# Gate projections moved from the output stage into attention, V products in groups, output stage pipelined deeper

## The chip, the core and the metric

The kernel runs on one core of a Trainium2 chip. The metric is device time in microseconds (us) of one execution, 4000.34 us before the change. TensorE multiplies matrices (PE in the profile; PEld is its loading of stationary operands), VectorE is DVE, ScalarE is ACT, GpSimd is POOL, and SyncE (SP) issues the DMAs.

## The reference, cut to what matters

Two layers of a mixer over 2048 latent and 256 context tokens of width 1024. A layer norms and modulates the stream, projects it, runs four branches of width 256 side by side, gates each by SiLU(z) of the same projection, and projects back:

```
h = rms_norm(x, g) * (1 + sc) + sh
(aq, ak, av, az, bq, bk, bv, bz, cu, cv, cz, dq, dk, dv, dz, drf, drb) = split(h @ w_in)
ya = rms_norm over heads of (softmax(q1 k1) - lam softmax(q2 k2)) v      # A: 4 heads
yb = softmax(q k) v, grouped queries                                     # B: 4 heads, 2 of k and v
yc = u * (w_s layer_norm(v) + b_s)                                       # C: in chunks of 128 tokens
yd = rms_norm(gated linear attention forwards + backwards)               # D
x  = x + gt * ([ya silu(az), yb silu(bz), yc silu(cz), yd silu(dz)] @ w_out)
```

The last layer gives no context output, and a final RMS norm follows.

## The kernel before, in words

All tokens are cut into 18 tiles of 128 (2 of context, 16 of latents; 34 tiles over both layers have an output, 18 and 16). Dense products are taken to float32's accuracy as three float32r products: `mm3` (lines 99 to 105) multiplies the two parts of h (hh, hl) with the two parts of a weight, over 8 row tiles, so 24 products per 512 columns. Each layer has four stages.

`proj_attn` and `proj_cd` compute h, q, k, v and the branches C and D but for D's backward scan; `pa_front` writes h to DRAM as `hT`, and `h_tile` (line 326) reads it back and splits it again into hh and hl, with a copy on ScalarE and a subtraction on VectorE (`split_tile`, line 284).

`attention` (line 743) goes through 4 rounds (a head of A together with one of B) of 8 blocks of 256 queries against all 2304 keys; in layer 0 each round has a small block for the context in front. `Slots` emits the work in slots, 18 per full block, in which blocks overlap. In a slot stands a score chunk of 768 keys: two products (`da_chunk`, line 845; `g_chunk`, line 883) into a PSUM tile s of two banks (two buffers), and one instruction of VectorE that reads it, keeps the scores of A and their running extreme. Then `da_exp` (858) exponentiates a whole row of 2304 on ScalarE, and `da_comb` subtracts the second softmax: 512 columns by ScalarE and POOL (871, 872), the others on VectorE in two pieces of 896 (875). In the slots of the next block follow `tr` (905, four transposes and a copy on ScalarE), `gs` (917 to 920, the transposed scores of B, an exponential on ScalarE, and a sum `acc` of them on POOL, 926), both through the PSUM tiles b (three buffers), and `pvm` (937), the V products: A's and B's halves write 64 partitions each, so they use 64 columns of TensorE's array (128*64 in the rows; other products have 128*128). One V product stands as four instructions in the trace. `o1` to `o3` scale and store a block's result `ot` (944 to 970). The order on TensorE is the scheduler's here: it places instructions by priority and its own cost model. SyncE's queue issues all loads in order; a load waits there for its buffer.

`output` (line 1070) takes the tiles in reverse, as D's backward scan does. Per tile it multiplies h with the gates' weights (two `mm3` of 512 columns, `pz`), norms A and D (`mixers`), multiplies with SiLU(pz) (`gates`), transposes (`turned`) and multiplies with w_out (two `mm3`, `po`, in `project`), which a tile later than the gates. TensorE's order is the order of the program there (`manual_schedule`). The first half of the gates' weights and the first tile of h are loaded while the last block of attention ends (1047 to 1059).

Of the kernel before, what the change touches and what calls it, by code (L numbers as in the profile page):

```python
# [9 lines left out]
F32 = mybir.dt.float32  # L10
F32R = mybir.dt.float32r
# [20 lines left out]
BIG = 3.0e38  # L32

# columns of the input projection
# [17 lines left out]
class Slots:  # L52
    """Emission in the order of slots, so that blocks overlap."""
# [17 lines left out]

class Kernel:
# [26 lines left out]
    def mm3(self, ps, hh, hl, wh, wl, c0, c1, ks=range(KT)):  # L99
        """ps = (hh + hl)^T (wh + wl) to float32's accuracy, over row tiles ks of KT."""  # L100
# [6 lines left out]
    def weights(self, wp, name, widths):  # L107
        """Tiles for the two parts of weights; the first are laid where a pool before frees its first."""
# [28 lines left out]
    # ---------------------------------------------------------------- all  # L137
    def run(self):
        tc, nc, I = self.tc, self.nc, self.I
        self.table()  # L140
        with ExitStack() as cx:
# [6 lines left out]
            # per layer: (1 + sc) g and sh by feature, lambda  # L148
# [16 lines left out]
            for i in range(DEPTH):  # L165
                d = {}
                for n, s in (
                    ("hT", [NTILE, P, KT * P]), ("aqk", [512, 2, NT]), ("bqk", [384, 2, NT]), ("v", [NT, 384]), ("o", [NT, 512]), ("c", [NT, 256]), ("od", [NT, 256]),
# [39 lines left out]
    # ---------------------------------------------------------------- modulation  # L208
    def ada(self, i, parts, wp, pp, start=False):
        """Shift (0), scale (1) and gate (2) of layer i, in steps of about a tile of weights."""  # L210
        nc, I = self.nc, self.I
        NB = 256
        if 2 in parts:
            # lambda, negated
# [11 lines left out]
        for r in parts:  # L226
# [33 lines left out]
            else:  # L260
                # rms_norm leaves out the factor 32 = sqrt(1024), which is put here
# [30 lines left out]
    def pa_load(self, i, t):  # L292
        """Tile t of the stream, normed (but for gains), and its rotary factors."""
# [12 lines left out]
    def pa_front(self, i, t, xn, pt, tag):  # L306
        """Tile t modulated and transposed, in two float32r parts."""
# [16 lines left out]
        nc.sync.dma_start(out=self.D[i]["hT"][t], in_=hT.rearrange("p k t -> p (k t)"))  # L324
        return self.split_tile(hT)

    def h_tile(self, i, t):
        """The same, from memory."""
        hT = self.xp.tile([P, KT, P], F32, name="hT", tag="hT", bufs=1)
        self.nc.sync.dma_start(out=hT.rearrange("p k t -> p (k t)"), in_=self.D[i]["hT"][t])  # L330
        return self.split_tile(hT)

    def pa_weights(self, i):
        """Weights of q and k of A, and of q, k and v of B."""
# [8 lines left out]
    def proj_attn(self, i, X, H, wcx, W):  # L343
        nc, I, D = self.nc, self.I, self.D[i]
        last = i == DEPTH - 1
        with ExitStack() as cx:
# [29 lines left out]
            for t in range(NTILE):  # L376
# [10 lines left out]
                def part_a():  # L387
                    """A: q, k"""
# [7 lines left out]
                def part_b():  # L396
                    """B: q, k, v"""
# [19 lines left out]
                def part_v():  # L417
                    """A: v"""
# [13 lines left out]
                else:  # L432
                    # the longer chain first
# [22 lines left out]
    def proj_cd(self, i, wc, first):  # L456
        nc, I, D = self.nc, self.I, self.D[i]
        last = i == DEPTH - 1
        with ExitStack() as cx:
# [19 lines left out]
            # C's constants  # L479
# [9 lines left out]
            # D's constants  # L489
            # rows: hi, hi and lo of the low-rank weights, hi and lo of the bias  # L490
# [30 lines left out]
            def stages(t, B):  # L521
                """The chain of one tile's D and C; each stage begins with work of TensorE."""
# [4 lines left out]
                # q, k and the decays' low-rank part, transposed  # L527
# [15 lines left out]
                # log-decays, both directions: min(z, 0) - ln(1 + exp(-|z|)); the 1 / 16 is in tri  # L543
# [11 lines left out]
                # their sums within the chunks: up to a token (transposed), and behind it  # L555
# [30 lines left out]
                # state increments of both directions, the forward scan  # L586
# [28 lines left out]
                # scores within the chunks, both directions  # L615
# [16 lines left out]
                if t % 2:  # L632
                    # C: the mix over the chunk's positions, two chunks at once
# [14 lines left out]
                # D: within the chunks, and from the state before  # L648
# [37 lines left out]
            # the chains of tiles without output are run behind, as they have less between their stages  # L686
# [55 lines left out]
    # ---------------------------------------------------------------- branches A and B  # L742
    def attention(self, i):
# [4 lines left out]
        CH, NCH = 768, 3  # L748
        with ExitStack() as cx:
            dcx = ExitStack()  # L750
            dp = dcx.enter_context(self.pool(f"dk{i}", 5, side="right"))
            qp = cx.enter_context(self.pool(f"qp{i}", 3))
            kp = cx.enter_context(self.pool(f"kp{i}", 2))
            ep = cx.enter_context(self.pool(f"ep{i}", 7))
# [584 lines left out]
```

## Time and profile before

| | |
|---|---|
| runs | 4000.34 us median of 3 (3998.8 to 4002.73) |
| span of the profiled execution | 4001.6 us, 67227 instructions; no other time of it is on the page |
| busy over the span | PE 3883.3 us (97%), DVE 2730.4 (68%), ACT 2322.1 (58%), POOL 1461.5 (37%) |
| DMA | 339.21 MB, mean 85 GB/s |
| mean granted clock of TensorE | 0.983 |

A layer's stages from the span's start: projections to 668 us, attention to 1640, output to 2062, projections to 2660, attention to 3605, output to the end. Busy times are unions of an engine's instructions. TensorE's instructions overlap each other in the records, so what one costs is read from the distance between the starts of two, not from its duration.

### The profile page before, as it was taken

The page shows a single profiled execution, that of the slowest core. Times are in us where ns is not written, and L with a number is a line of the kernel's source. Part 1 is how long each engine was busy: PE and PEld are TensorE (multiplying, and loading weights), DVE is VectorE, ACT ScalarE, POOL GpSimd, SP SyncE. Part 2 cuts the span into 40 slices and gives each one's busy share as a digit, 9 for nine tenths or more (in the row PEclk, how much of TensorE's full clock was granted, in tenths as well). Part 3 has the DMA queues.
Part 4 walks back from the last instruction along what each step waited for, and adds up shares of the span by engine and source line. Part 5 has one row for each costly group of instructions (what it writes and reads, how often), then busy time and mean ns, then how long its engine had stood idle before and what let it go on. Part 6 is the DMA issues. An engine that isn't in the chain of part 4 may idle for free.

```text
span 4001.6 us, 67227 instructions
## 1 busy us (share of the span) xinstructions
PE 3883.3 (97%) x24276; PEld 2877.1 (72%) x24276; DVE 2730.4 (68%) x6088; ACT 2322.1 (58%) x4181; POOL 1461.5 (37%) x1454
## 2 busy tenths in 40 slices
PE   7999998999999999999999999989999999999999
PEld 5888885666666666677878888866666666667777
DVE  5555545898989889533346654468999999976443
ACT  4434444677777777634444434447777777766554
POOL 1223221555555555311111132225555555552111
PEclk9999998999999999999999999979999999999999
DMA  8444334211020100533235431141111201015321
GB/s 265 148 150 133 115 99 111 65 41 43 22 67 21 33 24 24 182 103 104 94 120 179 143 119 56 60 106 49 45 34 29 56 21 31 22 50 169 103 95 58
DMA packets 302795, 339.21 MB, mean 85 GB/s; under 512 B 99384, under 2 KB 245760, under 8 KB 302464
## 3 DMA queue, kind: packets, MB, share of 16 engines
q1 hardware_dynamic: 302464, 334.92, 27.7%
q8 instruction: 192, 3.15, 0.3%
q14 instruction: 139, 1.14, 0.1%
HBM read 234.15 MB, written 100.62 MB: 84 GB/s over the span
## 4 chain that ended last, share of the span: by engine, by line
PE 87%; DMA 4%; DVE 4%; issue 2%; ACT 2%; POOL 1%; SPq 1%; DVEq 0%; POOLq 0%; ACTq 0%
PE pv L937 16%; PE s L845 8%; PE b L905 7%; PE b L917 5%; PE s L883 4%; PE b L918 3%; PE pz L103 3%; PE po L103 3%; PE po L105 3%; PE pz L105 3%; PE pz L104 3%; PE po L104 3%; PE pc L103 2%; PE pc L105 2%; PE pc L104 2%
## 5 line engine op out<-in xcount | busy, mean ns | idle before, releaser
L926 POOL TENSOR_TENSOR acc<-acc,gp 128x512 f32<-128x512 f32 x448 | 711.2, 1587 | 465.4 <-ACT gp L920 455.6
L937 PE MATMUL pv<-gp,v 128*64 128x256 f32 x2320 | 709.6, 400 | 0.0
L937 PE MATMUL pv<-wt,v 128*64 128x256 f32 x2320 | 709.2, 400 | 0.0
L858 ACT ACTIVATE e<-e,dm 128x2304 f32<-128x2304 f32 x256 | 568.7, 2221 | 48.3 <-DVE e L850 48.3
L850 DVE TENSOR_SCALAR_CACHE_REDUCE e<-s,dm 128x768 f32<-128x768 f32 x512 | 509.3, 1012 | 97.4 <-PE s L845 96.6
L845 PE MATMUL s<-dak,daq 128*128 128x384 f32 (+1 forms) x1568 | 461.8, 377 | 17.4 <-DMA daq<-aqk 7.4
L875 DVE SCALAR_TENSOR_TENSOR e<-e,r 128x896 f32<-128x896 f32 x256 | 457.8, 1808 | 0.1
L920 ACT ACTIVATE gp<-b 128x512 f32<-128x512 f32 x580 | 345.7, 596 | 100.5 <-PE b L918 87.9
L909 ACT COPY wt<-b 128x512 f32<-128x512 f32 x580 | 338.5, 585 | 112.5 <-PE b L905 99.0
L937 PEld LDWEIGHTS pv<-gp,v 128*64 128x64 f32 x2320 | 236.8, 135 | 205.8 <-issue 142.6
L905 PE MATMUL b<-ident,e 128*128 128x128 f32 x2304 | 360.7, 278 | 1.2 <-POOL e L872 1.2
L917 PE MATMUL b<-qa,ka 128*128 128x256 f32 x1160 | 354.2, 321 | 0.2
L905 PEld LDWEIGHTS b<-ident,e 128*128 128x128 f32 x2304 | 269.6, 141 | 93.7 <-issue 53.9
L845 PEld LDWEIGHTS s<-dak,daq 128*128 128x128 f32 x1568 | 247.7, 197 | 106.0 <-issue 85.5
L918 PE MATMUL b<-qb,kb 128*128 128x256 f32 x1160 | 305.5, 281 | 0.0
L917 PEld LDWEIGHTS b<-qa,ka 128*128 128x128 f32 x1160 | 220.7, 190 | 97.2 <-issue 71.6
L872 POOL TENSOR_TENSOR e<-e 128x512 f32<-128x512 f32 x128 | 171.2, 1337 | 306.5 <-ACT e L871 306.2
L888 DVE TENSOR_SCALAR_CACHE_REDUCE junk<-s,gm 128x768 bf16<-128x768 f32 x256 | 259.6, 1014 | 31.3 <-PE s L883 21.0
L850 DVE TENSOR_SCALAR_CACHE_REDUCE e<-s 128x768 f32<-128x768 f32 x256 | 239.6, 952 | 49.1 <-PE s L845 48.9
L1195 POOL TENSOR_TENSOR x<-x,g 128x512 f32<-128x512 f32 x66 | 88.8, 1345 | 427.1 <-DVE g L1193 406.4
L937 PEld LDWEIGHTS pv<-wt,v 128*64 128x64 f32 x2320 | 237.0, 135 | 0.6 <-issue 0.3
L883 PE MATMUL s<-ka,qa 128*128 128x384 f32 (+1 forms) x784 | 227.6, 373 | 9.1 <-DVE junk L888 6.2
(289 smaller groups left out, 9127.5 us busy)
## 6 DMA issues: line engine op xcount, KB each, us to landing
hT<-hT SPq DMA_DIRECT2D x104, 512.0 KB
dak<-aqk SPq DMA_DIRECT2D x96, 192.0 KB
daq<-aqk SPq DMA_DIRECT2D x136, 128.0 KB
wst<-in_w_in_dram SPq DMA_DIRECT2D x64, 256.0 KB
xa<-in_ada_w_dram SPq DMA_DIRECT2D x32, 512.0 KB
bst<-bst SPq DMA_DIRECT2D x68, 194.0 KB
xa<-xb SPq DMA_DIRECT2D x19, 512.0 KB
v<-v SPq DMA_DIRECT2D x16, 576.0 KB
```

The costliest lines, as they stand in the source:

```text
L845: nc.tensor.matmul(s[:, u, :hc], lhsT=Q["daq"][m][:, qt * P : (qt + 1) * P], rhs=R["dak"][m][c][:, u * hc : (u + 1) * hc], start=True, sto ...
L850: nc.vector.tensor_scalar(out=E[qt, m][:, c * ch : (c + 1) * ch].rearrange("p (u f) -> p u f", u=2), in0=s[:, :, :hc], scalar1=-SC, scalar ...
L858: nc.scalar.activation(e, e, AF.Exp, bias=NM[qt, m], scale=-1.0, accum_out=L[qt][:, m : m + 1])
L875: nc.vector.scalar_tensor_tensor(out=E0[:, a : a + w], in0=E1[:, a : a + w], scalar=RR[qt][:, 2:3], in1=E0[:, a : a + w], op0=ALU.mult, op ...
L883: nc.tensor.matmul(s[:, u, :hc], lhsT=Q["QA"][:, qt * P : (qt + 1) * P], rhs=R["KA"][c][:, u * hc : (u + 1) * hc], start=True, stop=True,)
L905: nc.tensor.transpose(s[:, j * 256 + qt * P : j * 256 + (qt + 1) * P], W[qt][:, k * P : (k + 1) * P], ident)
L909: nc.scalar.copy(WT[u], s)
L917: nc.tensor.matmul(o, lhsT=R["KA"][k // 6][:, ks], rhs=Q["QA"], start=True, stop=False)
L918: nc.tensor.matmul(o, lhsT=R["KB"][k // 6][:, ks], rhs=Q["QB"], start=False, stop=True)
L920: nc.scalar.activation(g, s, AF.Exp, scale=0.125)
L926: nc.gpsimd.tensor_tensor(out=B["acc"], in0=B["acc"], in1=g, op=ALU.add)
L937: nc.tensor.matmul(B["pv"][o : o + 64, :256], lhsT=R["V"][:, k, o : o + 64], rhs=x[:, js], start=k == 0, stop=k == nkt - 1,)
```

## The change

The gates' products become a generator, `gates`, which goes through the four branches' weights (256 columns each) and all output tiles, and yields after every product of 256 columns; each finished piece is copied out by ScalarE and stored in DRAM as `z`. A class `Pace` draws from it: at two places in each slot of attention, `fill` takes products until a counted cost reaches `rate` times the slot. The counts (352 for a chunk, 432 for `tr`, 472 for `gs`, 432 for `pvm`, 119 for a gate product) are nanoseconds. h is stored in DRAM as its two parts (`hs`), and `h_tile` reads these without splitting.

In attention TensorE now follows the program's order. V products are emitted in four groups per block, of the pairs of key tiles (0, 1), (2, 3), (4, 5) and (6, 7, 8). The combination is wholly VectorE's, in four pieces; the exponential goes in two halves of a row; the four scalings of a result become one instruction. The PSUM tiles b have two buffers instead of three, as `pz` takes a bank. Buffers of k, v and the score rows are fewer, v comes in halves, loads stand elsewhere in their slots, and a round's blocks run from the last to the first. The first half of w_out is loaded at the end of attention.

The output stage reads z, applies SiLU from SBUF, and lets `mixers` run two tiles ahead of `project`; `turned` has two pairs of buffers, `po` three banks.

```diff
@@ new, beside Slots
+STEP = 119
+class Pace:
+    def __init__(self, steps, n, slots, cost):
+        self.steps, self.left, self.cost, self.rest = steps, n, 0, 0
+        self.rate = (n * STEP + cost) / slots
+    def fill(self, slot):
+        if slot < 3 or slot < self.rest:
+            return
+        for _ in range(8):
+            if not self.left or self.cost >= self.rate * slot:
+                return
+            self.step(slot)
+    def step(self, slot):
+        if next(self.steps) is None:
+            self.rest = slot + 1
+            return
+        self.left -= 1
+        self.cost += STEP
@@ h_tile
-        hT = self.xp.tile([P, KT, P], F32, name="hT", tag="hT", bufs=1)
-        self.nc.sync.dma_start(out=hT.rearrange("p k t -> p (k t)"), in_=self.D[i]["hT"][t])
-        return self.split_tile(hT)
+        h = []
+        for z, n in enumerate(("hh", "hl")):
+            h.append(self.xp.tile([P, KT, P], F32R, name=n, tag=n))
+            self.nc.sync.dma_start(out=h[z].rearrange("p k t -> p (k t)").bitcast(F32), in_=self.D[i]["hs"][t, :, z])
+        return h
@@ attention
-            pb = cx.enter_context(self.pool(f"pb{i}", 3, PSUM))
+            pb = cx.enter_context(self.pool(f"pb{i}", 2, PSUM))
+            pz = cx.enter_context(self.pool(f"pz{i}", 1, PSUM))
+            cx.enter_context(self.tc.manual_schedule(engines={PE}))
...
+                    pace.cost += 352 if full else 120
...
-                def da_exp(qt, m):
-                    e = E[qt, m][:, :nk]
-                    nc.scalar.activation(e, e, AF.Exp, bias=NM[qt, m], scale=-1.0, accum_out=L[qt][:, m : m + 1])
+                def da_exp(qt, m, b):
+                    w = nk // 2
+                    e = E[qt, m][:, b * w : (b + 1) * w]
+                    nc.scalar.activation(e, e, AF.Exp, bias=NM[qt, m], scale=-1.0, accum_out=L[qt][:, b, m : m + 1])
...
-                        if npl:
-                            nc.scalar.activation(E1[:, :npl], E1[:, :npl], AF.Copy, scale=r[:, 2:3])
-                            nc.gpsimd.tensor_tensor(out=E0[:, :npl], in0=E0[:, :npl], in1=E1[:, :npl], op=ALU.add)
...
-                    for qt in range(2):
-                        for o, sc in ((0, RR[qt][:, 0:1]), (64, rl[:, 2 * qt : 2 * qt + 1])):
-                            dst, src = ob[:, qt, o : o + 64], op[:, qt * P + o : qt * P + o + 64]
-                            nc.vector.tensor_scalar(out=dst, in0=src, scalar1=sc, scalar2=None, op0=ALU.mult)
+                    nc.vector.tensor_tensor(
+                        out=ob.rearrange("p t (b d) -> p t b d", d=64),
+                        in0=B["op"][:, 0:256].rearrange("p (t b d) -> p t b d", t=2, d=64),
+                        in1=bc(B["r"][:, :, 0:2], [[4, 2], [1, 2], [0, 64]]), op=ALU.mult,
+                    )
...
-                        S.at(s + 1 + 2 * m, lambda qt=qt, m=m: da_exp(qt, m), -1)
-                    npt = 2 if full else 1
+                        for b in range(2):
+                            S.at(s + 1 + 2 * m + b, lambda qt=qt, m=m, b=b: da_exp(qt, m, b), -1)
+                    npt = 4 if full else 1
...
+                for z in range(int(base), int(s)):
+                    S.at(z, lambda z=z: pace.fill(z), 3)
+                    S.at(z, lambda z=z: pace.fill(z + 0.5), 9)
...
-                        for j in range(2):
-                            S.at(b0 + 2 * u + 5.5 + j, lambda u=u, j=j: pvm(u, j), 5)
+                    for us in ((0, 1), (2, 3), (4, 5), (6, 7, 8)):
+                        for u in us:
+                            for j in range(2):
+                                S.at(b0 + 2 * us[-1] + 5.5, lambda u=u, j=j: pvm(u, j), 5)
...
-                for b in range(8):
+                for b in reversed(range(8)):
+            pace = Pace(self.gates(i, fp, pz), 24 * 4 * (NTILE if with_ctx else NTILE - CTILE), 32 * 18 + with_ctx * 12, 32 * 25200 - 17000)
@@ new
+    def gates(self, i, fp, pz):
...
+        def load():
+            t, b = halves[len(loaded)]
+            h = fp.tile([P, 2, KT // 2, P], F32R, name="fh", tag="fh", bufs=3)
...
+        for n, (g, t) in enumerate(units):
+            ps = pz.tile([P, 512], F32, name="pz", tag="pz")
+            for k in range(KT):
+                if k % 4 == 0 and len(loaded) < len(halves):
+                    load()
+                h = loaded[2 * n + k // 4]
+                w = W[g, k]
+                for z, (a, b) in enumerate(((0, 0), (0, 1), (1, 0))):
+                    nc.tensor.matmul(
+                        ps[:, :256], lhsT=h[:, a, k % 4], rhs=w[:, b], start=k == 0 and z == 0, stop=k == KT - 1 and z == 2
+                    )
+                    yield 1
+                if t == tiles[-1] and g < 3:
+                    weight(g + 1, k)
+            zs = fp.tile([P, 256], F32, name="zs", tag="zs", bufs=2)
+            nc.scalar.copy(zs, ps[:, :256])
+            nc.sync.dma_start(out=D["z"][t * P : (t + 1) * P, g * 256 : (g + 1) * 256], in_=zs)
+            yield None
@@ output
-                self.mm3(B["pz"][0], hh, hl, *Wz[0], 0, 512)
...
+            chain(0)
+            turned(T[0])
+            chain(1)
+            chain(2)
+            for k, (n, b) in enumerate(steps):
+                if k + 1 in firsts.values():
+                    turned(T[steps[k + 1][0]])
+                if b == 0 and n > 0:
+                    chain(n + 2)
+                project(T[n], b)
```

`chain(n)` is `mixers` of tile n and the scan and loads of the next; `steps` are the pairs (tile, half of w_out).

## Rows read from the trace of the kernel before

**Rows 1.** Busy time of each engine by stage; instructions in brackets, then clock, DMA.

```profile
330.00:668.00 338.00, 331.60 (x2747) 268.17 (x2746) 168.56 (x520) 157.63 (x482) 90.69 (x202) 1.00 0.33 107
668.00:1640.00 972.00, 948.58 (x6196) 628.95 (x6196) 846.37 (x1676) 687.99 (x1055) 505.86 (x365) 0.98 0.17 45
1640.00:2062.00 422.00, 418.10 (x1944) 331.93 (x1944) 172.75 (x391) 188.77 (x251) 77.86 (x118) 0.99 0.34 112
...
3605.00:4001.00 396.00, 383.08 (x1768) 302.10 (x1768) 183.32 (x438) 209.16 (x296) 70.66 (x108) 0.98 0.32 105
```

The busy times are in the order PE, PEld, DVE, ACT, POOL.

**Rows 2.** The same for ten blocks of layer 1's attention.

```profile
2800.00:3083.30 283.30, 282.18 (x1882) 188.75 (x1884) 257.34 (x493) 207.69 (x310) 158.99 (x111) 1.00 0.13 35
```

**Rows 3.** Groups by line, same ten blocks: busy us, mean ns, idle before.

```profile
L875 DVE SCALAR_TENSOR_TENSOR e<-e,r 128x896 f32<-128x896 f32 x40 | 74.3, 1876 | 0.0
...
L964 DVE TENSOR_SCALAR ob<-b,rl 128x64 f32<-128x64 f32 x20 | 5.5, 274 | 0.0
...
L858 ACT ACTIVATE e<-e,dm 128x2304 f32<-128x2304 f32 x40 | 88.9, 2222 | 4.2 <-DVE e L850 4.2
...
L909 ACT COPY wt<-b 128x512 f32<-128x512 f32 x90 | 52.6, 585 | 14.5 <-PE b L905 12.1
...
L944 ACT COPY ot<-pv 128x256 f32<-128x256 f32 x10 | 3.7, 373 | 3.5 <-PE pv L937 3.5
```

**Rows 4.** TensorE's timeline, 3000 to 3029.6 us: start, duration, instruction.

```profile
3001.07 0.43 PE L937 MATMUL pv<-gp,v 128*64 128x256 f32 x1
...
3002.53 0.38 PE L937 MATMUL pv<-gp,v 128*64 128x256 f32 x1
...
3002.75 0.38 PE L937 MATMUL pv<-gp,v 128*64 128x256 f32 x1
...
3010.49 0.53 PE L845 MATMUL s<-dak,daq 128*128 128x384 f32 x2
3010.85 0.28 PE L917 MATMUL b<-qa,ka 128*128 128x256 f32 x1
3010.97 0.27 PE L918 MATMUL b<-qb,kb 128*128 128x256 f32 x1
3011.18 0.43 PE L937 MATMUL pv<-gp,v 128*64 128x256 f32 x1
...
3011.76 0.63 PE L845 MATMUL s<-dak,daq 128*128 128x384 f32 x2
3012.22 0.60 PE L905 MATMUL b<-ident,e 128*128 128x128 f32 x4
...
3026.58 0.43 PE L937 MATMUL pv<-gp,v 128*64 128x256 f32 x1
```

**Rows 5.** TensorE's timeline in an output stage and in a projection stage.

```profile
1849.98 0.39 PE L104 MATMUL pz<-zl,hh 128*128 128x512 f32 x1
...
1855.09 0.40 PE L105 MATMUL pz<-zh,hl 128*128 128x512 f32 x1
...
2499.89 0.28 PE L103 MATMUL pqk<-cwh,hh 128*128 128x256 f32 x1
...
2500.84 0.28 PE L105 MATMUL pqk<-cwh,hl 128*128 128x256 f32 x1
```

**Rows 6.** Groups by line on ScalarE, layer 1's output stage.

```profile
L288 ACT CAST hh<-hT 128x1024 fp32r<-128x1024 f32 x15 | 15.6, 1041 | 0.0
```

**Rows 7.** The chain that ended last, end of layer 0's attention: start, us, what.

```profile
1634.92 4.49 DMA wst<-in_w_in_dram
```

**Rows 8.** Line 875's instructions in layer 1: duration in ns, min/median/max.

```profile
L875 DVE SCALAR_TENSOR_TENSOR e<-e,r x128: 1139/2054/2181, 2679.1 to 3579.1; 128x896 f32<-128x896 f32 x128
```

**Rows 9.** Timelines of POOL and VectorE, 2821.5 to 2827 us.

```profile
2822.07 1.30 POOL L872 TENSOR_TENSOR e<-e 128x512 f32<-128x512 f32 x1 [2.48 <-ACT e L871]
...
2822.13 4.26 DVE L875 SCALAR_TENSOR_TENSOR e<-e,r 128x896 f32<-128x896 f32 x2
```

**Rows 10.** Waits of SyncE's queue in layer 0's attention: us, times, longest.

```profile
SPq L818 <- PE s L845: 308.5, 24, 14.4
```

More of the change, by code (lines that the diff above doesn't have):

```diff
@@ L69, in run, with begin, drain @@
                 f()
+class Pace:
+    def __init__(self, steps, n, slots, cost):
+        self.steps, self.left, self.cost, self.rest = steps, n, 0, 0
+        self.rate = (n * STEP + cost) / slots
+    def begin(self):
+        next(self.steps)
+    def fill(self, slot):
[11 more added lines that the diff above has]
+        self.cost += STEP
+    def drain(self):
+        for _ in self.steps:
+            pass
 class Kernel:
@@ L837, in da_chunk @@
                         E[qt, m] = (
[L838 removed]
+                            ep.tile([P, NT], F32, name=f"e{m}", tag=f"e{m}", bufs=4 - 2 * m) if full
                             else ep.tile([P, 256], F32, name="ec", tag="ec", bufs=5)
@@ L880, in g_chunk @@
                 def g_chunk(qt, c):
+                    pace.cost += 352 if full else 120
                     s = pf.tile([P, 2, 512], F32, name="s", tag="s")
@@ L900, in tr @@
                 def tr(u):
+                    pace.cost += 432
                     s = pb.tile([P, 512], F32, name="b", tag="b")
@@ L911, in gs @@
                 def gs(u):
+                    pace.cost += 472
                     s = pb.tile([P, 512], F32, name="b", tag="b")
@@ L932, in pvm @@
                     k = 2 * u + j
+                    pace.cost += 432
                     if k == 0:
@@ L1022, in attention @@
                 ld_dak(R, c)
+            pace.begin()
             for c in range(with_ctx, NCH):
                 ld_ka(R, c)
-            ld_v(R)
+            for c in range(2):
+                ld_v(R, c)
             for bi, (r, q0, nk) in enumerate(blocks):
@@ L1046, in attention @@
                 base = end
+            pace.drain()
             dcx.close()
@@ L1070, in output @@
-    def output(self, i, zcx, Wz, turn):
+            gcol = hp.tile([P, 2], F32, name="gcol")
+            lam_init = 0.8 - 0.6 * math.exp(-0.3 * i)
+            for j, n in enumerate(("da_subln_g", "gla_norm_g")):
+                for o in (0, 64):
+                    nc.sync.dma_start(out=gcol[o : o + 64, j : j + 1], in_=self.I[n][i].rearrange("(p o) -> p o", o=1))
+            nc.vector.tensor_scalar(out=gcol[:, 0:1], in0=gcol[:, 0:1], scalar1=1.0 - lam_init, scalar2=8.0, op0=ALU.mult, op1=ALU.mult)
@@ L1071, in output, with out_weights @@
+    def out_weights(self, i, W, b, gcol, stage=None):
+        for k in range(KT):
+            col = gcol[:, 0:1] if k < 2 else gcol[:, 1:2] if k >= 6 else None
+            src = self.I["w_out"][i, k * P : (k + 1) * P, b * 512 : (b + 1) * 512]
+            self.split_weights(W[0][:, k, :], W[1][:, k, :], [src], 512, col, stage)
+    def output(self, i, zcx, Wo, gcol):
         nc, I, D = self.nc, self.I, self.D[i]
         last = i == DEPTH - 1
-        lam_init = 0.8 - 0.6 * math.exp(-0.3 * i)
@@ L1172, in turned, with project @@
                     nc.vector.tensor_tensor(out=yl[:, ks], in0=p3, in1=yh[:, ks].bitcast(F32), op=ALU.subtract)
-            def project(t, B, mid=None):
+            def project(B, b):
+                t = B["t"]
                 s = 1 if t < CTILE else 0
                 ts = slice(t * P, (t + 1) * P)
+                end = last and t == outs[-1]
                 if s not in gts:
@@ L1229, in output @@
[L1229 to L1250 removed]
+            bsts = [scan(t) for t in order[: order.index(outs[0]) + 1]][-1:]
@@ new lines, in output, with chain @@
+            T = [load(t) for t in outs[:2]]
+            Wo = Wo + self.weights(wo, "ob", [512])
+            self.out_weights(i, Wo[1], 1, gcol)
+            cx.enter_context(self.tc.manual_schedule(engines={PE}))
+            def chain(n):
+                if n < NO:
+                    mixers(bsts[n], T[n])
+                if n + 1 < NO:
+                    bsts.append(scan(outs[n + 1]))
+                    if n + 1 >= len(T):
+                        T.append(load(outs[n + 1]))
+            steps = [(0, 0), (1, 0), (0, 1), (1, 1)]
@@ new lines, in output @@
+            tail = 0 if last else 2
+            steps += [(n, b) for n in range(2, NO - tail) for b in range(2)]
+            if tail:
+                steps += [(NO - 2, 0), (NO - 1, 0), (NO - 2, 1), (NO - 1, 1)]
+            firsts = {n: k for k, (n, b) in enumerate(steps) if b == 0}
+            chain(0)
+            turned(T[0])
+            chain(1)
+            chain(2)
+            pw = None
+            for k, (n, b) in enumerate(steps):
[4 more added lines that the diff above has]
+                project(T[n], b)
+                if not last and (n, b) == (NO - 1, 0):
+                    zcx.close()
+                    pw = self.pa_weights(i + 1)
+                    self.tc.keep_in_program_order(self.table())
+                    X, H = {t: self.pa_load(i + 1, t) for t in range(2)}, {}
+                if not last and (n, b) == (NO - 2, 1):
+                    H[0] = self.pa_front(i + 1, 0, X[0][0], pt, "py")
```

225 lines of the change are left out of this document (92 added, 133 removed).

## The prediction, made before the changed kernel was run

> **What bounds the kernel now.** I read the table of stages first. TensorE is busy in 948.6 of the 972 us of layer 0's attention, VectorE in 846.4; in the two output stages TensorE is busy in 418.1 of 422 and 383.1 of 396 us, and no other engine in much over half [rows 1]. So the question is what TensorE spends its time on. Ten blocks of attention (a block is 256 queries of one head) make it plain: ten copies of a block's result in 283.30 us are 28.33 us a block, of which TensorE is idle 0.11 and VectorE 2.6 [rows 2, 3]. TensorE sets the period.
>
> But 28.33 us is not all products. In the timeline a score chunk's two products take 0.36 us (3010.49 to 10.85) and a 256-column product 0.12 (to 10.97) [rows 4]. A V product is four instructions; within a run of them the pairs start 0.22 apart, so one V product is worth 0.43 us [rows 4]. Alone it costs more: before it the last product takes 0.21 instead of 0.12 (to 11.18), the four hold TensorE for 0.58 (to 11.76), and the next chunk takes 0.46 instead of 0.36 (to 12.22) [rows 4]. That is 0.09 + 0.15 + 0.11 = 0.35 us, I use 0.345, for every entry into the 64-column form and return. One period of the timeline has 15 such entries, the first at 3001.07 and the last at 3026.58: thirteen of one V product, one of two, one of three [rows 4]. All products at their spacings within runs come to 23.2 us, and 15 x 0.345 = 5.2: together 28.4 against the 28.33 of the period.
>
> **The change part by part.** The sum is made against the profiled span, 4001.6 us, which lies 1.3 above the runs' median.
>
> Gate products leave the output stage: 34 tiles x 48 products of 512 columns. The 23rd starts 5.11 us after the first [rows 5], 0.232 each: -378.6 us. What lay behind them comes up. A tile then has 418.1/18 - 11.1 = 12.1 us of TensorE. ScalarE was busy 209.2/16 = 13.1 us per tile in layer 1 [rows 1], of which the split of h, 1.04 [rows 6], goes: 12.0, as long as TensorE. I add 0.4 us per tile, +14, between nothing and 1.5 (+51). The first tile's norms have no gate products in front any more, some +8 per layer (up to 15); the wait for the first gate weights, 4.49 [rows 7], goes, and the one for the last attention output behind it, as the blocks now run backwards and the first output tile is done early. I take zero, between -16 and +30.
>
> They come back in attention: 34 x 96 products of 256 columns. Eight steps of such a stream take 0.95 us [rows 5], 0.119 each: +388.4 us. Twice the instructions on half the columns cost 10 us more.
>
> V products come in four groups per block instead of 15 entries: 64 blocks x 11 x 0.345 = -242.9 us. This is the gain.
>
> TensorE alone thus makes 4001.6 - 378.6 + 388.4 - 242.9 = 3768.5 us, and a block without gates 28.33 - 3.80 = 24.53 us.
>
> Can the other engines follow? Pace releases gate products by a budget of 1.69 us per slot (18 slots a block), against 22.25 / 18 = 1.24 that it counts for attention itself. So 0.456 us, 3.8 gate products, go into a slot. With a credit of 15.9 us for the first block, which has only scores, they are used up after (205.6 - 15.9) / 0.456 = 416 slots, 23 blocks, in layer 0, and after 20.5 in layer 1. That makes 43.5 blocks of 24.53 + 8.2 = 32.75 us and 20.5 without gates.
>
> VectorE per block: 25.73 busy now [rows 2]. Of the combination it has 896 of each 1152 columns, 4 x 1.876 = 7.5 [rows 3]; ScalarE and POOL have the rest. With all of it on VectorE there are 8 pieces of 576. One of 896 takes 1.14 at the least [rows 8], so a piece some 0.78 (part of it is fixed); at the present mean per column it is 1.21. The timeline shows what stretches them: a POOL addition of 1.30 starts at 2822.07, two pieces at 2822.13 need 4.26 for 2 x 1.14 [rows 9], so each waits an addition out. POOL keeps eight or nine of them, busy near half the block, so I take 0.78 plus 0.45 x 0.64 of waiting: 8.6 in all, between 6.2 and 9.7. The result's four scalings of 0.27 [rows 3] become one of four times the columns, about 0.42: -0.66; small additions +0.3. Together 26.5, between 24.1 and 27.6.
>
> The Trainium skill, SBUF — State Buffer, section "SBUF: two separate sides", calls the ports that the two engines share an exclusive lock, held for a whole instruction. This trace agrees (4.26 for 2.28). It speaks against the change: by it a short piece waits as long as a long one, so pieces cut in eight wait up to twice as often as four; it is behind the fourth rival.
>
> In the 43.5 blocks with gates VectorE's 26.5 and ScalarE's 21 to 23 (20.8 now [rows 2], less 1.4 of scaling, more read-outs and gate copies) lie below 32.75. Locally they don't: a slot with half a softmax costs ScalarE 2.22/2 + 0.3 of start and read-out + 0.59 of a copy [rows 3] = 2.0, one with a combination piece VectorE 1.08 + 0.9 of a chunk (the rest of its 25.73, over 18) = 2.0. TensorE has 1.82 per slot, its order is now written by hand, and its transposes have two banks instead of three. Two chunks of buffer take up most: I add 0.7 us a block, +30, between 0 and 14 heavy slots x 0.2 = 2.8 (+122).
>
> In the 20.5 without gates TensorE needs 24.5 and VectorE 26.5: VectorE becomes the bound. With 1.5 us of idle time (2.6 now) that is 28.0, no gain over 28.33: +71, between 0 and 31.0 us, three more of idle (+133).
>
> Other edits at nothing: h is stored and read as two parts, 0.5 MB more per tile each way. Where it is read, TensorE has 331.6/18 = 18.4 us of products per tile beside it, at a DMA share of 0.33 [rows 1]; if they didn't cover it, 2 to 3 us a tile would show there. The first block's gate products fill idle time of TensorE but wait for their own first loads.
>
> Forecast: 3768.5 + 14 + 0 + 30 + 71 = 3884 us.
>
> **The rivals.**
> 1. TensorE stays the only bound: 3768. For it: 0.11 us of idle time per block now [rows 2]. Against: VectorE's 26.5 in blocks of 24.5. Gates that spread over all blocks, unlike my reading of the budget, would come close to it: blocks of 24.53 + 6.07 = 30.6 stay above VectorE, some 3800.
> 2. Slower: the V groups have no cover. Between groups the chunks run at the pace of VectorE and ScalarE (14 heavy slots of 2.05 us); in a group of 2.1 to 2.9 us TensorE delivers no scores, and the others have at most two chunks to work off. If a group hid nothing, a block with gates took 28.7 + 4 light slots x 1.26 + 9.2 = 42.9; each hides up to a slot, 2.05, so 34.7, and 32.9 without gates. That is 43.5 x 34.7 + 20.5 x 32.9 = 2184 against 1813 now: +371 - 379 + 14, no change. So it decides from the point where a group hides less than one slot; at 0.9 of one (0.8 us more per block) the time is 4060. Against: softmax pieces of 2.2 us [rows 3] cost TensorE nothing today, though its planned order may be why.
> 3. Late loads: a half tile of h (512 KB) is needed every 12 gate products, 5.7 us, on a queue that stood 308.5 us waiting for TensorE in this stage [rows 10]. At 0.43 us late for each of the 272 halves the forecast's gain is gone; at 0.6 late it is 4050.
> 4. All eight pieces wait for a whole addition: 8 x (0.78 + 1.28) = 16.5, VectorE 34.4 in every block; 64 x 34.4 - 1813 = +389, less 365: 4026. POOL's ten additions would each have to start just ahead of a piece.
>
> **How the numbers follow.** The forecast 0.60 (its own range 3825 to 3950), the first rival with the even spreading 0.22, the second 0.10, the third 0.04, the fourth 0.03, others 0.01. From 3755, a little below TensorE's sum as waits at the stage ends may go, to 3990, below the break-even of rival 2, lies 0.8. A measurement of this kernel can tell about 0.2%, 8 us, from no change: faster 0.82, within it 0.03, slower 0.15.
>
> **What would show it.** Output stages of 12.1 to 12.6 us a tile (some 220 and 205 us); blocks of 33 to 34 us in the first two thirds of attention and about 28 in the last third, where TensorE has idle time that ends with VectorE's chunks; four runs of V products per block with edges of 0.35; gate products 0.119 apart, and none after 23 and 20 blocks. Wrong it is if blocks average over 34.0 us, if TensorE waits for h by DMA, or if the last blocks keep to 24.5.

## The result, and the profile of the changed kernel

The changed kernel takes 4233.8 us (median of 4 runs, 4229.9 to 4241.6), 1.0586 times the time before (95% interval 1.0571 to 1.0601). The forecast was 3884 and the range ended at 3990: it is slower by 233 us where I said faster by 116. The profiled span is 4230.0 us, TensorE's mean granted clock 0.963 (0.983 before), its busy time 3802.2 us (90%).

First the stages. The columns are those of [rows 1]: window, length, busy time of PE, PEld, DVE, ACT, POOL, then clock, DMA share and GB/s.

```profile
661.00:776.00 115.00, 71.55 (x420) 62.87 (x421) 42.59 (x105) 29.69 (x70) 6.05 (x11) 0.75 0.73 211
776.00:1545.00 769.00, 703.41 (x5266) 582.94 (x5264) 545.60 (x1108) 458.69 (x870) 230.15 (x185) 0.99 0.41 125
1545.00:1915.00 370.00, 325.12 (x2240) 241.78 (x2238) 296.71 (x594) 244.89 (x448) 138.35 (x109) 0.96 0.11 31
1915.00:2200.00 285.00, 247.76 (x1240) 192.20 (x1236) 160.22 (x414) 127.69 (x192) 84.38 (x129) 0.93 0.55 182
...
3974.00:4225.00 251.00, 212.27 (x1030) 163.51 (x1030) 170.39 (x436) 145.27 (x225) 75.05 (x111) 0.92 0.46 156
```

The output stages are short, nearly as forecast: from one tile's first `po` to the next it is 12.8 us in layer 0 and 13.4 on average in layer 1 (forecast 12.1 to 12.6). Attention is not. From the first score to the last V product it takes 1247.5 and 1193.1 us, 282.7 and 257.5 more than before; the forecast's terms gave +247 for both layers together. And TensorE, busy in 948.6 of 972 us before [rows 1], now idles in every part of it: 43 us of the first 115, 66 of the next 769, 45 of the last 370.

Two stretches of layer 1, fifteen blocks with gates and ten without, answer to [rows 2]:

```profile
2953.20:3513.90 560.70, 514.75 (x3845) 426.99 (x3843) 404.71 (x796) 332.63 (x614) 171.04 (x137) 0.99 0.42 125
3584.00:3888.90 304.90, 269.44 (x1878) 201.83 (x1877) 265.70 (x520) 208.07 (x369) 116.43 (x90) 0.99 0.10 27
```

With gates a block takes 37.4 us (32.75 of products by the forecast), without 30.5 (24.5). VectorE is busy 26.6 us of the latter, TensorE 26.9: neither is full. Who waits for whom stands in the groups by line (busy us, mean ns, idle before and its releaser), here of TensorE in the ten blocks without gates; the same two lines had no idle time before:

```profile
L888 PE MATMUL s<-dak,daq 128*128 128x384 f32 x240 | 70.1, 374 | 17.5 <-DVE e L893 17.5
...
L927 PE MATMUL s<-ka,qa 128*128 128x384 f32 x120 | 36.8, 388 | 10.5 <-DVE e L893 9.5
```

In the fifteen with gates TensorE is idle for 46 us, and half of that stands before products into the single bank `pz`, which wait for ScalarE's copy `zs` of the finished unit (24 products). The copy takes 0.37 us, and the next unit's first product starts 0.05 us behind it.

```profile
L1153 PE MATMUL pz<-fw,fh 128*128 128x256 f32 x1025 | 168.4, 293 | 22.9 <-ACT zs L1160 22.7
```

Last, the start of attention, in the chain of what ended last (start, us, what). TensorE waits for halves of h there; eight gate products take 0.95 us, as forecast.

```profile
707.91 6.40 DMA fh<-hs
...
723.12 7.93 DMA fh<-hs
...
741.11 8.48 DMA fh<-hs
...
762.10 0.95 PE pz L1153 x8
```

The first V product comes 106.4 and 99.9 us after the first score (47.5 and 38.1 before), with 278 and 277 gate products, 33 us, ahead of it.

### The profile page after: what moved, and what is told of

Same layout as the page of the kernel before. It is cut to its first block, busy times and chain, and to the rows that moved or that the text cites. A ratio compares the mean times of both kernels' runs of the same rounds, so it can differ in the third digit from the quotient of the medians.

```text
span 4230.0 us, 71935 instructions
## 1 busy us (share of the span) xinstructions
PE 3802.2 (90%) x25908; PEld 3071.1 (73%) x25908; DVE 2721.8 (64%) x6272; ACT 2229.8 (53%) x4595; POOL 1187.8 (28%) x1326
## 4 chain that ended last, share of the span: by engine, by line
PE 61%; DVE 17%; DMA 7%; issue 6%; ACT 6%; SPq 1%; POOL 1%; ACTq 0%; DVEq 0%; POOLq 0%
PE pv L984 9%; PE pz L1153 7%; DVE e L893 5%; PE b L950 4%; DVE e L918 4%; PE s L888 3%; PE s L927 3%; DVE junk L932 3%; PE po L134 2%; DMA fh<-hs 2%; PE po L136 2%; PE po L135 2%; PE b L963 2%; PE b L964 2%; PE pc L134 2%
## 5 line engine op out<-in xcount | busy, mean ns | idle before, releaser
L972 POOL TENSOR_TENSOR acc<-acc,gp 128x512 f32<-128x512 f32 x448 | 593.8, 1325 | 1095.2 <-ACT gp L966 1088.1
L902 ACT ACTIVATE e<-e,dm 128x1152 f32<-128x1152 f32 x512 | 642.4, 1256 | 77.8 <-DVE e L893 74.5
L1153 PE MATMUL pz<-fw,fh 128*128 128x256 f32 x3264 | 545.9, 298 | 142.5 <-ACT zs L1160 73.1
L1153 PEld LDWEIGHTS pz<-fw,fh 128*128 128x128 f32 x3264 | 463.7, 196 | 176.9 <-ACT zs L1160 102.3
L984 PE MATMUL pv<-gp,v 128*64 128x256 f32 x2320 | 565.8, 389 | 0.0
L984 PE MATMUL pv<-wt,v 128*64 128x256 f32 x2320 | 565.8, 389 | 0.0
L918 DVE SCALAR_TENSOR_TENSOR e<-e,r,e 128x576 f32<-128x576 f32 x512 | 467.3, 935 | 3.9
L984 PEld LDWEIGHTS pv<-gp,v 128*64 128x64 f32 x2320 | 299.9, 138 | 169.7 <-issue 22.1
L963 PE MATMUL b<-qa,ka 128*128 128x256 f32 x1160 | 313.2, 292 | 30.0 <-DVE ob L1006 12.6
L984 PEld LDWEIGHTS pv<-wt,v 128*64 128x64 f32 x2320 | 299.9, 138 | 0.0
```

The lines of the kernel that those rows point to most:

```text
L902: nc.scalar.activation(e, e, AF.Exp, bias=NM[qt, m], scale=-1.0, accum_out=L[qt][:, b, m : m + 1])
L918: nc.vector.scalar_tensor_tensor(out=E0[:, a : a + w], in0=E1[:, a : a + w], scalar=RR[qt][:, 3:4], in1=E0[:, a : a + w], op0=ALU.mult, op ...
L963: nc.tensor.matmul(o, lhsT=R["KA"][k // 6][:, ks], rhs=Q["QA"], start=True, stop=False)
L972: nc.gpsimd.tensor_tensor(out=B["acc"], in0=B["acc"], in1=g, op=ALU.add)
L984: nc.tensor.matmul(B["pv"][o : o + 64, :256], lhsT=R["V"][k // VH][:, k % VH, o : o + 64], rhs=x[:, js], start=k == 0, stop=k == nkt - 1,)
L1153: nc.tensor.matmul(ps[:, :256], lhsT=h[:, a, k % 4], rhs=w[:, b], start=k == 0 and z == 0, stop=k == KT - 1 and z == 2)
```

## The experiments

All times are medians of 4 or 5 runs beside runs of the kernel before (3998 to 4002 us on every occasion). "By hand" means TensorE's order in attention as in the change; "the planner" is the scheduler that orders it in the kernel before.

**Pacing, with the order by hand.** The first edit spreads the gates over all blocks, the second starts `Pace` with 24 us already on its count, so that the first block gets fewer, and `k3_heven` has both.

```diff
-            pace = Pace(..., 32 * 25200 - 17000)
+            pace = Pace(..., 32 * 22500 - 17000)        # e1_even (k3_heven: + 7000)
-        self.steps, self.left, self.cost, self.rest = steps, n, 0, 0
+        self.steps, self.left, self.cost, self.rest = steps, n, 24000, 0   # e2_first, k3_heven
```

> Only the budget of Pace is lower, so that the gate products last to the end of attention instead of two thirds of it. Theory: the changed kernel (4234 us) loses time because TensorE, in an order written by hand, stands behind VectorE and ScalarE; blocks without gate products already stand 5.7 of their 30.2 us, and gate products put there fill the standing time. Then 19 such blocks give back about 4 us each: some 4160. Rival: the standing time belongs to the gate products themselves (their loads, their one PSUM bank), so it moves with them: 4234.

> Pace starts with 24 us on its count, so that nearly no gate product is released before the first V product. Theory of late loads at the start: the time from the first score product to the first V product, 106 and 100 us now against 47 and 38 before the change, falls back to about 50 and 40; the 555 gate products that ran there (66 us) come later, half of them into the standing time of the blocks at the end: some 4160. Rival: the first blocks are slow for another reason (score buffers, fewer buffers of k): the two stay near 100 and the time near 4234.

> The changed kernel, TensorE's order still by hand, with both of the pacing edits together (gates over the whole of attention, and none before the first slots' worth of other work). It is the kernel of 3981 us but for the written order, so the two tell what the order costs at the same pacing. Theory (order and pacing are separate costs; the pacing edits alone gave 43 and 36 us): 4234 - 79 = 4155 us, the order then costs 174. Rival (with even pacing gate products cover the written order's waits for VectorE, so the order costs little): 4050 us or less.

Measured: 4190.4, 4197.8 and 4165.3 us (the last 1.0412 times the kernel before, 1.0396 to 1.0427). Alone they are worth 43 and 36 us, about half of what their theories gave; together 68, near the theory of `k3_heven`. In `e2_first` 76 and 75 gate products stand ahead of the first V product, which comes at +68.6 and +63.0. Pacing is a part of the loss, not all of it.

**The bank of the gates.** `e3_rest` was to make the next unit begin a slot later; `f1_copy` issues the copy directly behind the 24th product, with the same rest.

```diff
-            self.rest = slot + 1
+            self.rest = slot + 2        # e3_rest
@@ step, f1_copy
+        if self.left % 24 == 0:
+            next(self.steps)
+            self.rest = slot + 1
```

> After each finished piece of the gates Pace rests two slots instead of one before it writes the same PSUM bank again. Theory: in blocks with gates TensorE stands 2.1 us each for ScalarE's copy out of that bank; that goes: 43 x 2.1 = 90 us, some 4145. Rival: ScalarE or VectorE is late anyway, and the wait moves to the next product: within 20 us of 4234.

> The changed kernel with one edit: the copy of a finished gate unit out of its bank is issued directly behind the unit's 24th product instead of just ahead of the next unit's first, and the next unit begins one slot (half a period of about 2 us) later. Theory (TensorE stands for that copy about 2.05 us in each of some 43 blocks with gates, because there is one bank and the copy is issued at the last moment): 4233.8 - 43 x 2.05 = about 4146 us, blocks with gates 35.4 us instead of 37.4. Rival (the time only moves to the next wait in the order, that for VectorE's minimum): 4220 to 4234.

Measured: 4230.1 us, within the runs of the changed kernel, and 4217.0, 17 less. But neither took the wait away. In TensorE's waits from 815 to 1350 us (total, times, longest) it is 24.1 us in the changed kernel, and in `f1_copy` still

```profile
PE pz L1156 <- ACT zs L1163: 22.1, 31, 1.5
```

and in 32 of 41 units the next one's first product still starts within 0.1 us of the copy's end (38 of 41 in the changed kernel and in `e3_rest`). The code says why: `fill` looks at `rest` only where it begins, and not in its loop, so the draw that ends a unit goes on to the next one's first product while the count allows it. The rest never stood between the copy and that product in these units, and what the wait is worth by itself neither run shows.

**VectorE's work.** 2/9 of the combination back to ScalarE and GpSimd, as before the change:

```diff
...
+            nc.scalar.activation(E1[:, :npl], E1[:, :npl], AF.Copy, scale=r[:, 3:4])
+            nc.gpsimd.tensor_tensor(out=E0[:, :npl], in0=E0[:, :npl], in1=E1[:, :npl], op=ALU.add)
...
```

> ScalarE and POOL again do two ninths of the combination, as before the change. Theory: VectorE, 26.4 us busy per block, sets the 30.2 us of the blocks without gates; it is relieved by some 2 us: these blocks come to 28.5, blocks with gates gain 0.5: some 4180. Rival: POOL's additions then hold VectorE up again, or TensorE's order and not VectorE's load sets the blocks: within 20 us of 4234.

Measured: 4244.6 us, as its rival said. The run relieves VectorE of little: in ten blocks without gates its busy time falls from 26.6 to 25.7 us a block, and the period by as much, from 30.5 to 29.6; most blocks with gates get longer. So it does not settle what VectorE's load costs where there are no gates. VectorE isn't full in these blocks, in either kernel: it is idle for 3.9 us of each.

**The order.** `e6_auto` takes the order by hand out of the change, `f3_hand` puts it alone into the kernel before, `f2_group` puts the V groups alone there, `f4_both` both; `e5_single` takes the groups out of the change.

```diff
-            cx.enter_context(self.tc.manual_schedule(engines={PE}))      # e6_auto; + in f3_hand, f4_both
-                    for us in ((0, 1), (2, 3), (4, 5), (6, 7, 8)):       # e5_single; + in f2_group, f4_both
-                        for u in us:
-                            for j in range(2):
-                                S.at(b0 + 2 * us[-1] + 5.5, lambda u=u, j=j: pvm(u, j), 5)
...
```

> The changed kernel with the V products issued one by one again, two slots apart as in the kernel before, instead of in four groups a block. Theory (the groups save what they were costed at, 0.345 us an entry, also under the written order): about 11 to 14 more entries a block, 64 blocks: 4234 + 243 to 309 = 4477 to 4543 us. Rival (TensorE stands in these blocks anyway, and the groups make it stand longer since they pile up work on one bank): 4180 to 4300.

> The changed kernel without the written order on TensorE in attention, so that the planner orders it; it keeps 8.5 entries of V products a block where the written order has 4.1. Theory (TensorE's waits of about 4.6 us a block with gates and 2 to 3 us a block without come of an order that can't go round a late operand): they fall by two thirds, -43 x 3.1 - 20 x 2 = -173, the entries cost 64 x 4.4 x 0.345 = +97, about 4158 us. Rival (the planner has no better order, since one bank for gates, two for scores and two for the rest are the limit): 4234 + 97 = 4330 us or more.

> The kernel before with two parts of the change alone: V products in four groups a block, and TensorE's order in attention written by hand. Gates stay in the output stage. Theory of the prediction (groups are worth 64 x 11 x 0.345 = 243 us and the rest of the order costs little): about 3760 to 3830 us. Rival (the written order brings its own waits, as in the changed kernel's blocks without gates, 30.2 us each where TensorE works 26.7 of it): 64 blocks at 30 us against 29.7 now, so 4000 to 4040 us.

> The kernel before with V products issued in four groups a block and nothing else; its planner still orders TensorE and lets 10.75 entries of V products a block stand where the kernel before has 15.25. Theory (a group is worth 0.345 us an entry, and it is the written order that loses it): 64 x 4.5 x 0.345 = -99, about 3901 us. Rival (the groups themselves make TensorE wait, whoever orders it): 3990 to 4070 us.

> The kernel before with TensorE's order in attention written by hand (the slots' order) and nothing else; V products stay single, 18.0 entries a block instead of 15.25. Theory (the written order makes TensorE wait about 3.3 us a block that the planner fills): 64 x (3.3 + 2.7 x 0.345) = +271, about 4270 us. Rival (the waits come of the groups, not of the order): 64 x 0.93 = +60, 4060 us.

Measured: `e5_single` 4331.6 us, between its two expectations, and `e6_auto` 4085.7 (1.0212, 1.0196 to 1.0227), below its theory. In the kernel before, with the period of a block of layer 1 and the entries into V products in it as counted in the trace:

| | V products single | in groups |
|---|---|---|
| planner | 4000 us; 28.33, 15.0 entries | 3948.1 (0.9867, 0.9852 to 0.9881); 27.35, 10.0 entries |
| by hand | 4220.1 (1.0540, 1.0522 to 1.0557); 32.2, 18.0 entries | 4068.9 (1.0169, 1.0153 to 1.0184); 29.2, 4.0 entries |

`f2_group` lies midway between its theory and its rival, `f4_both` beyond its rival, `f3_hand` 50 below its theory. The order by hand costs 220 us with single products and 121 with groups, in a kernel without any gates in attention, and 148 in the changed one. The kernel before keeps its three PSUM buffers b and has no `pz` there, so the cost doesn't hang on the fewer buffers of the change. The groups are worth 53 us with the planner, 151 by hand, 98 in the changed kernel: they are no loss. Ten blocks of `f4_both`, then of `f2_group`:

```profile
2900.00:3192.70 292.70, 263.91 (x1888) 200.77 (x1886) 257.57 (x491) 209.38 (x312) 146.22 (x112) 1.00 0.17 44
```

```profile
2800.00:3073.40 273.40, 267.63 (x1881) 193.65 (x1881) 251.41 (x491) 205.57 (x311) 152.43 (x111) 1.00 0.16 42
```

The same products, with TensorE idle in 28.8 us of the one and 5.8 of the other. `f4_both`'s groups by line say why, TensorE's first, then VectorE's:

```profile
L846 PE MATMUL s<-dak,daq 128*128 128x384 f32 x240 | 68.8, 368 | 12.8 <-DVE e L851 12.8
...
L884 PE MATMUL s<-ka,qa 128*128 128x384 f32 x120 | 36.9, 388 | 12.5 <-DVE e L851 11.6
```

```profile
L851 DVE TENSOR_SCALAR_CACHE_REDUCE e<-s 128x768 f32<-128x768 f32 x40 | 36.6, 951 | 25.2 <-PE s L846 25.2
```

TensorE waits for VectorE's reading of scores, and VectorE waits for TensorE's scores: they stand by turns. In the timeline (start, us, instruction, idle time before) VectorE gets two combination pieces in a row, 4.02 us, and only then reads the next scores. TensorE, whose next instruction by the order is a score chunk, stands for 1.28 us, from the last of these pieces to the end of that reading (3022.34). A little later TensorE runs 24 instructions of V products in a row, and VectorE stands for 2.51:

```profile
3020.45 0.68 PE L906 MATMUL b<-ident,e 128*128 128x128 f32 x4
3022.41 0.61 PE L846 MATMUL s<-dak,daq 128*128 128x384 f32 x2 [1.28 <-DVE e L851]
...
3025.71 0.43 PE L938 MATMUL pv<-gp,v 128*64 128x256 f32 x1
...
3028.14 0.38 PE L938 MATMUL pv<-wt,v 128*64 128x256 f32 x1
```

```profile
3017.46 4.02 DVE L876 SCALAR_TENSOR_TENSOR e<-e,r 128x896 f32<-128x896 f32 x2
3021.40 0.94 DVE L851 TENSOR_SCALAR_CACHE_REDUCE e<-s 128x768 f32<-128x768 f32 x1
...
3029.50 0.96 DVE L851 TENSOR_SCALAR_CACHE_REDUCE e<-s 128x768 f32<-128x768 f32 x1 [2.51 <-PE s L846]
```

With single products by hand the pair changes: in ten blocks of `f3_hand` the largest wait is that of the transposes in `qb`, put right behind the last score chunk.

```profile
2900.00:3222.00 322.00, 300.16 (x1887) 186.74 (x1886) 252.68 (x492) 209.02 (x312) 151.69 (x111) 0.98 0.12 30
...
L897 PE MATMUL b<-ident,mz 128*128 128x128 f32 x20 | 5.7, 286 | 17.8 <-DVE junk L889 17.8
```

So it isn't one bad place: each order by hand has waits of its own.

**The gates with the planner and even pacing.**

`g1_aeven` is `e6_auto` with the pacing of `k3_heven`; `g2_acopy` adds the copy of `f1_copy` to it, `k1_aoff` the edit of `e4_off`, `k2_late` a slower pace, `k4_lateoff` the last two.

```diff
-            pace = Pace(..., 32 * 22500 + 7000)                              # g1_aeven
+            pace = Pace(..., 32 * 22500 - 21600 - 20000 * (not with_ctx))    # k2_late
```

> The changed kernel with TensorE in attention left to the planner, gates paced over the whole of attention (not over its first two thirds), and none before the first slots' worth of other work. Theory (with the planner TensorE is busy 96 to 97% wherever there are gates, so blocks of 29 us with TensorE at 92% are waste): 43.5 blocks at 35.0 and 20.5 at 29.0 become 64 at 32.6, -33, and the start of attention falls by about 20: about 4033 us. Rival (the blocks without gates were no loss, as VectorE bounds them): 4075 to 4095 us.

> As the one with the planner, even pacing and no early gates, but the copy of a finished gate unit is issued directly behind its last product. Theory (the wait for the single bank, 0.7 us a unit, is the largest local wait left): 136 units x 0.5 = -68 against that one. Rival (the planner already moves other products into that wait; e.g. only 0.2 us a unit is seen with it): within 10 us of that one.

> The kernel of 3981 us (planner, even pacing) with 2/9 of the combination of scores given back to ScalarE and GpSimd, as in the kernel before. Theory (VectorE is no limit once its blocks of 26.4 us of work lie in blocks of 32.6): 3975 to 3987 us. Rival (TensorE's last waits are for VectorE's minima, some 0.4 us a block, and they go): 3955 us.

> The kernel of 3981 us with the pacing slowed further, so that some 250 gate products of the first layer and some 330 of the second are left for the end of attention and the start of the output stage, where TensorE now has some 30 us and 36 us with little work. Theory (they fill that idle time): attention's blocks get shorter by 30 us and 39 us, about 3912 us. Rival (left over products run in a row, each unit behind the copy of the last, ahead of the output's first turn): 3960 to 3985 us.

> Both of the last two edits together. Theory: the sum of the two, 3905 to 3915 us. Rival: 3960 to 3985 us.

Measured: `g1_aeven` 3981.2 us (0.9949, 0.9935 to 0.9964), better than its theory; `g2_acopy` 3979.4, its rival. In the window of the fifteen blocks above `g1_aeven` has seventeen, with 900 gate products, and TensorE idles in 11.7 us instead of 46:

```profile
2953.20:3513.90 560.70, 548.96 (x4127) 454.46 (x4127) 463.24 (x911) 372.88 (x689) 199.44 (x157) 1.00 0.37 115
```

`k1_aoff` missed both: 4136.5 us, 155 more. TensorE's idle time before score products of A, 7.3 us in this window of `g1_aeven`, is there

```profile
L887 PE MATMUL s<-dak,daq 128*128 128x384 f32 x376 | 112.5, 373 | 30.1 <-DVE e L892 30.1
```

Pieces of the combination stand four in a row on VectorE, with nothing between them for TensorE's scores:

```profile
3011.78 4.50 DVE L921 SCALAR_TENSOR_TENSOR e<-e,r,e 128x448 f32<-128x448 f32 x4
```

Such rows are not new, 56 of them here and 46 in `g1_aeven`, but they take 4.43 us on average where `g1_aeven`'s, of longer pieces, take 3.55; the last section has what stretches them. That they make up all of the 155 us is not shown.

`k2_late` took 4015.0 us, beyond even its rival. In layer 1 blocks fall to about 31 us, but the gate products left over don't lie beside the end of attention: from the last score to the last V product it takes 75.1 and 88.2 us (31.1 and 29.5 in `g1_aeven`), and the first product of the output stage comes 37.4 and 36.1 later, as without the edit. They wait for h by DMA once more, and TensorE's granted clock is 0.83 there (3671 to 3795 us):

```profile
L1152 PE MATMUL pz<-fw,fh 128*128 128x256 f32 x312 | 42.7, 289 | 10.4 <-DMA fh<-hs 9.6 <-ACT zs L1159 0.5
```

`k4_lateoff`, 4166.9 us, has both losses and misses both of its expectations.

Of all these the best is `f2_group`, 3948 us: one part of the change, alone.

## Why the prediction was wrong

Two pairs cross: order and pacing, each with the gates moved. By hand it is 4234 with the change's pacing and 4165 with even pacing; with the planner 4086 and 3981. The order costs 148 or 184 us, the pacing 68 or 105, so neither is the other in disguise. They are not wholly separate: from `g1_aeven` on they are 184 and 105 one by one, and 253 together, so 36 us are counted in both. The 233 us can be walked in measured steps, though the size of a step depends on what was changed ahead of it: groups -53 (4000 to 3948), gates moved and the rest of the change +33 (3981), the change's pacing +105 (4086), the order by hand +148 (4234).

**The step that failed** is the pair of waits, "I add 0.7 us a block, +30, between 0 and 14 heavy slots x 0.2" and "With 1.5 us of idle time (2.6 now) that is 28.0". I had priced the order by hand as overflow of single slots, small because "Two chunks of buffer take up most", though its instructions can't go round a late one. Measured, blocks with gates stand 4.6 us above their products, and blocks without are 30.5 us, at the far end of my range. Over 43.5 and 20.5 blocks that is an estimated 320 us where the two terms have 101; some 50 of it belong to the entries below. That VectorE would set the period of the latter was also wrong: in `f4_both`, with VectorE's old work, they are 29.2. The evidence that the planner hid such waits was in [rows 2]: 0.11 us of idle time per block on TensorE with VectorE at 91%. I read it as proof that the waits were small; it was the planner's work, since the same kernel by hand (`f3_hand`) is idle on TensorE for 2.2 us a block, as the second rival half says of the softmax pieces ("though its planned order may be why").

**The V groups**, -243, were mis-sized. An entry is worth less than 0.345: from 15.0 to 10.0 entries the period fell by 0.98 us while idle time grew by 0.46, so 0.29 each; from 18.0 to 4.0 by hand, 3.0 and 0.7, 0.26. Eleven entries then give about 190. By hand 14 go, some 230 us at 0.26, of which 151 came in the kernel before and 98 in the changed one; that the rest went into waits fits the idle time, and no run shows it by itself. With the planner a third of the entries went, since it takes groups apart again.

**The gates' products** were right: 0.119 us each, and with planner and even pacing moving them, with the rest of the change, costs +33 where the same terms of the forecast (-378.6 + 388.4 + 14) make +24. No run moves the gates alone. This exchange was never a gain by itself.

**The pacing** I computed nearly rightly (the last gate product follows the scores of 21.7 and 20.0 full blocks, forecast 23 and 20.5) but priced only through VectorE. It leaves blocks of two kinds, and TensorE idles in both.

**The stage ends**, taken as zero, cost more. The gate products of the first block didn't fill idle time: they stand in a row, 26 to 29 us later per layer than their own 33 us account for, behind loads of h. This is the third rival's mechanism, but only there. From the last V product to the end of the layer's output and the next projections it is 164.6 and 149.5 us less than before, 314 against 365 in the forecast's terms. The missing 50 us have three parts: some 17 from tiles 12.8 and 13.4 us apart instead of 12.5; some 22 from a start that takes 37 and 36 us from the last V product to the first output product, as before (35 and 37), although 11 us of gate products a layer are gone from it; and 10 in layer 1's projections, where TensorE waits 8.2 us for the first reload of the two parts of h, which the forecast put at nothing. By the forecast such a wait was to show in every tile, if at all; it shows once.

**The rivals.** The second, groups without cover at 4060, describes `f4_both` (4069) and its waits on both sides; but the groups win even there, so its price belongs to the order, and it had a chance of 0.10. The first is refuted by 8 to 12% idle time on TensorE, and its even spreading, some 3800, by the 4165 of `k3_heven`; the fourth by pieces of 0.94 us on average.

What stays open: which neighbours in the slots' order would have to part for the order by hand to equal the planner's, what a second bank for the gates would be worth, and why `f3_hand` loses 3.9 us a block when its recorded idle time and three more entries explain only 2.9.

## What to carry to other kernels

An engine at 99% under a scheduler that may reorder tells nothing of its waits under a written order: price the order by itself, and try it alone. Move work beside other work only where the receiving stage has idle time on the bound engine; otherwise it is an exchange, here of 365 us for 388 in the forecast's terms. Spread such work evenly and not from the first moment: that was worth 68 us by hand and 105 with the planner.

## What the runs showed of the hardware

Giving part of VectorE's work to GpSimd made VectorE's remaining instructions longer. In the window of `k1_aoff` a combination piece of 448 columns takes 997 ns on average, in that of `g1_aeven` one of 576 takes 926:

```profile
L921 DVE SCALAR_TENSOR_TENSOR e<-e,r,e 128x448 f32<-128x448 f32 x128 | 122.3, 997 | 0.8
```

```profile
L917 DVE SCALAR_TENSOR_TENSOR e<-e,r,e 128x576 f32<-128x576 f32 x140 | 124.3, 926 | 1.0
```

Alone the shorter is 0.67 us (at 3001.44); the four in 4.50 us stand from 3011.78 on, and GpSimd's additions run at 3012.64 and 3014.16. Counted over the whole execution of `k1_aoff`, the 162 pieces with no addition of GpSimd beside them take 0.67 to 0.69 us, the 121 with two beside them 1.65 on average. So here work that went from VectorE to GpSimd came back as waiting. This agrees with the Trainium skill, SBUF — State Buffer, section "SBUF: two separate sides", by which the two engines share a pair of ports under an exclusive lock.

TensorE's granted clock was 0.75 over the first 115 us of the changed kernel's attention, a mean between its two levels (1.2 and 2.4 GHz), where it stood 32.2 us for loads of h and was busy 71.6 us; in the stretch behind, busy 703.4 of 769 us, it was 0.99, nearly all at the upper level.
